# Values and latents paired with gates in two passes of seven half-block products, their weights' sums added up in place by transfers

## The chip, the cores and the metric

The kernel runs on one core of one Trainium2 chip. The metric is the device time of one execution in microseconds (us). Times and profiles come from the chip: the profiler records one execution, and the runs are timed apart from it.

Five engines take part: TensorE (PE, matrix products into PSUM), VectorE (DVE), ScalarE (ACT), GpSimd (POOL) and SyncE (SP). Each runs its own list of instructions in order and stops at the first whose semaphores are not there yet. SP issues nearly all loads; POOL issues the transfers that add to what lies at their target. Sixteen DMA engines move the data.

## The reference: what is computed

One decoder layer on 512 tokens of width 2048, in float32. A normalised input is multiplied by one wide weight, whose columns make all the parts:

```python
h = _rms_norm(x, g_pre)
proj = h @ w_in
(q_lat, kv_lat, k_rope_raw, gate_mla,
 fq, fk, fv, f_logit, gate_fox) = jnp.split(proj, split_points, axis=-1)
o_mla = _mla_branch(q_lat, kv_lat, k_rope_raw, ..., cos, sin) * jax.nn.silu(gate_mla)
o_fox = _fox_branch(fq, fk, fv, f_logit, b_forget) * jax.nn.silu(gate_fox)
o = jnp.concatenate([o_mla, o_fox], axis=-1) @ w_out
return x + _rms_norm(o, g_post)
```

Eight FoX heads (width 128, with forget gates) work on `fq`, `fk`, `fv`, each 1024 wide. Eight MLA heads get their queries, keys and values by a second projection (`w_uq`, `w_ukv`) out of the normalised latents (768 and 512 wide); 64 values of each query and of one shared key are turned by rotary angles, `positions` times a frequency. Both branches are multiplied by SiLU gates of 1024 columns each.

## The kernel before

**Products.** Each float32 number is split into a high part that TensorE takes whole and a low rest, and a product is three matmuls: high by high, high by low, low by high (`mm3`, lines 149 to 152). `h` (`hh`, `hl`) stays in SBUF. Weights come in chunks of 512 KB (128 partitions by 1024 columns, two 128-row blocks of 512 columns or four of 256). `chunk` keeps loads some chunks ahead (`load`, L259 for plain ones, L242 for summed ones); `divide` makes the high part on ACT (`whi`, L279) and the rest on DVE (`wlo`, L282). All chunks of a stage share three places of raw weights in the pool `wp`, with some more in other pools.

**Seven products for eight.** For several groups of columns the product of 2 by 2 half-blocks is done by seven products of sums (names `p1`, `p2`, `p4`, `q6`, `g7`, `g5`, `g3`) in place of eight; `p` ones take blocks of `h`, the others sums of blocks of `h`, which are made once, stored in DRAM (`awaymg`) and fetched again (`bmg`, `bmq`). Before the change these are the FoX values (v), the latents (l), the MLA gates (m), the up-projection (u) and the output (o). The FoX gates are four plain passes, `fg`. The latents are computed turned (weights on the stationary side, so 128 columns by 256 tokens come out and no transposes are wanted later); the MLA gates are not, and are turned afterwards by 32 transposes `gmt`.

**Sums of weights.** A seven-product also wants sums of weight blocks. They are made in DRAM ahead of time: `add_step` copies a block to DRAM with SP (`t7v`, `t6v`, ...) and adds a second one with an accumulating transfer of POOL (L320), paced by `set_pace`. Others are joined on DVE: the second block is loaded beside the first (`second`) and added (`raw<-raw,second`, L269).

**Order.** The start is written out by hand: `proj_first` turns the tokens of `x` (`xt`, by TensorE), makes `h` out of them (ACT the high part, DVE the low part, L145) and uses each of the 16 rows k of `h` at once in the product `in` (L614). `x` and the first weights come in by SP in the order in which they are used. After that a planner orders each engine's instructions by its own estimate of when operands are there, save where `in_order` pins them; smaller work is handed out between the steps of products from a list, `todo`. The rotary tables are such a list: about 25 DVE operations of 128x512, the first of them pinned (L838), in the passes of FoX gates and values.

Of the kernel before, what the change touches and what calls it, by code (L numbers as in the profile page):

```python
# [12 lines left out]
F32 = mybir.dt.float32  # L13
# [6 lines left out]
P = 128  # L20
# [27 lines left out]
DEEP, EXTRA = 6, 3  # L48
# [18 lines left out]
def tile_hybrid_layer(  # L67
# [69 lines left out]
    def split_into(hi, lo, src, scale=None, pin=False):  # L137
        if scale is None:
            a = act.copy(hi, src)
            b = dve.tensor_tensor(out=lo, in0=src, in1=hi.bitcast(F32), op=ALU.subtract)  # L140
            if pin:
                in_order(a, b)
        else:
            act.mul(hi, src, scale)
            dve.scalar_tensor_tensor(  # L145
                out=lo, in0=src, scalar=scale, in1=hi.bitcast(F32), op0=ALU.mult, op1=ALU.subtract
            )

# [70 lines left out]
    raws, ready, up_chunks, early = {}, {}, set(), set()  # L219

    more, deep, seconds = [], [], [vr, 2]
    needs = {}

    def raw_tile(i):
        if deep and deep[1] <= i < deep[2] and (i - deep[1]) % (DEEP + 3) < DEEP:
            return deep[0].tile([P, 1024], F32, tag="raw", name=f"raw{i}", bufs=DEEP)
        if i in up_chunks:
            return slot(f"raw{i}", shape=(P, 1024))
        if i <= prods["g7", "v"][-1] and i % 5 < 2:
            return vr.tile([P, 1024], F32, tag="raw", name=f"raw{i}", bufs=2)  # L230
        pool = more[0] if more and (i - more[1]) % 6 < 3 else wp
        return pool.tile([P, 1024], F32, tag="raw", name=f"raw{i}", bufs=3)

    def load(i, small=None):

        w, cols, k, n, width = chunks[i]
        assert state["step"] >= needs.get(i, -3) + 2
        if cols is None:
# [5 lines left out]
            if k is not None:  # L244
                if seconds and i not in early:
                    pool, bufs = seconds
                    second = pool.tile([P, 2, 512], F32, tag="second", name=f"second{i}", bufs=bufs)
                else:
                    second = slot(f"second{i}")
# [22 lines left out]
    def divide(i):  # L272
# [6 lines left out]
        cast = act.copy(hi[:, :m], raw[:, :m])  # L279
        if deep:  # L280
            tc.keep_in_program_order(cast)
        dve.tensor_tensor(out=lo[:, :m], in0=raw[:, :m], in1=hi[:, :m].bitcast(F32), op=ALU.subtract)  # L282
        ready[i] = [t[:, :m].rearrange("p (k c) -> p k c", k=n) for t in (hi, lo)]

# [7 lines left out]
    def chunk(i, ahead_load=4, ahead=2):  # L292
        upto = i + ahead_load
        if deep:
            upto = max(upto, min(i + DEEP + 2, deep[2] - 1, state["loaded"] + i % 2))
# [4 lines left out]
        for k in range(i + ahead + 1, min(state["loaded"], i + ahead + (3 if deep else 2))):  # L300
            join(k)
# [63 lines left out]
    AT = {"v": O_FV, "l": 0, "m": O_GM}  # L365
# [5 lines left out]

    for g in "vlm":
        sum_blocks(g, lambda j, h, c, g=g: in_block(g, j, h, c), ("t4", "t5"))
# [16 lines left out]
    for n in ("g0", "p1", "g1", "p2", "g2", "s5", "q0", "s3", "k0", "s6", "p4", "s7",  # L390
              "q1", "k1", "q2", "k2", "q3", "k3", "g3"):
        name = {"p1": "p1", "p2": "p2", "p4": "p4", "s5": "g5", "s3": "g3", "s6": "q6", "s7": "g7"}.get(n)
        if name:
            add_products([(name, "v")], plain_in)
            if n == "s5":
                early.update(prods["g5", "v"][2:])
        else:
            at = {"q": O_FQ, "k": O_FK, "g": O_GF}[n[0]] + 256 * (3 - int(n[1]))
            fox[int(n[1])][n[0]] = add_chunks(w_in, [(0, at, 256)], NK, 4, 256)
    add_products(  # L400
        [
            ("p1", "l"), ("p1", "m"), ("p2", "l"), ("p4", "l"), ("p2", "m"), ("p4", "m"),
            ("q6", "l"), ("g5", "m"), ("g7", "l"), ("g5", "l"), ("g3", "l"),
            ("q6", "m"), ("g7", "m"), ("g3", "m"),
        ],
        plain_in,
    )
    mla = [{} for _ in range(4)]
    for n in ("q0", "p1", "k0", "q6", "p2", "p4", "g7", "q1", "g5", "k1", "g3", "q2", "k2", "q3", "k3"):
# [6 lines left out]
        if n[0] == "q":  # L416
            mla[p]["q"] = add_chunks(
                w_uq,
                [
                    (0, 2 * QK * p, NOPE),  # L420
# [1458 lines left out]
```

## Time and profile before

Three runs gave 893.46, 893.65 and 896.54 us; the median is 893.65 us. The profiled execution has a span of 892.3 us.

| what | before |
|---|---|
| span of the profiled execution | 892.3 us |
| median of the runs | 893.65 us |
| TensorE busy | 880.3 us (99%), 4486 matmuls and transposes |
| DVE busy | 660.2 us (74%) |
| ACT busy | 462.1 us (52%) |
| POOL busy | 72.8 us (8%) |
| moved by DMA | 225.07 MB |

Busy time is the share of the span in which an engine had an instruction running; matmuls overlap, so the mean duration of one (some 0.39 us for 128x512) is longer than the distance from one start to the next. That distance is what a matmul costs here, and it is read from the timeline. "PEclk" is the clock granted to TensorE. A window's DMA share is the mean busy share of 16 engines.

### The profile page before, as it was taken

How to read it: one execution, taken by the hardware profiler on the slowest of the kernel's cores; microseconds unless marked ns; L12 is line 12 of the kernel's file. 1: busy time of each engine (PE TensorE's matmuls, PEld its weight loads, DVE VectorE, ACT ScalarE, POOL GpSimd, SP SyncE). 2: the span in 40 equal slices, each digit the busy share in tenths (PEclk: the TensorE clock that was granted, in tenths of full speed). 3: DMA queues.
4: the chain of work that ended last, by engine and by line, in shares of the span. 5: the costliest groups of instructions: out<-in, count | busy, mean ns of one | idle time of the engine just before them, and what ended most of it. 6: DMA issues, size and time to landing. Idle time of an engine off the chain costs nothing.

```text
span 892.3 us, 12700 instructions
## 1 busy us (share of the span) xinstructions
PE 880.3 (99%) x4486; PEld 748.2 (84%) x4486; DVE 660.2 (74%) x1106; ACT 462.1 (52%) x841; POOL 72.8 (8%) x92
## 2 busy tenths in 40 slices
PE   9999999999999999999999999999999999999996
PEld 9988887888888888888998999788888888888885
DVE  4579995648665546477678999979787895988786
ACT  6944434334343433335455565657465776646383
POOL 0110110011110211010000000000000000000021
PEclk9999999999999999999999999999999999999999
DMA  9998798889999999997799885697988637799878
GB/s 319 277 265 241 212 341 279 250 214 315 261 282 275 238 230 225 247 231 186 243 412 410 329 303 178 167 275 166 221 182 215 153 111 233 228 323 322 264 214 254
DMA packets 139235, 225.07 MB, mean 252 GB/s; under 512 B 16898, under 2 KB 68892, under 8 KB 138148
## 3 DMA queue, kind: packets, MB, share of 16 engines
q1 hardware_dynamic: 124660, 184.19, 63.5%
q0 software_dynamic: 13776, 39.85, 22.2%
q8 instruction: 35, 0.57, 0.2%
q10 hardware_dynamic: 736, 0.22, 0.1%
q14 instruction: 28, 0.23, 0.1%
HBM read 209.53 MB, written 69.22 MB: 312 GB/s over the span
## 4 chain that ended last, share of the span: by engine, by line
PE 91%; DVE 4%; DMA 2%; ACT 2%; issue 1%; DVEq 0%; ACTq 0%; SPq 0%
PE fq L150 3%; PE fk L150 3%; PE fk L152 3%; PE fk L151 3%; PE fq L152 3%; PE fq L151 3%; PE fg L150 3%; PE in L614 3%; PE fg L151 3%; PE fg L152 3%; PE sm L657 3%; PE mq L152 2%; PE mq L150 2%; PE mq L151 2%; PE oa L150 2%; PE oa L152 2%
## 5 line engine op out<-in xcount | busy, mean ns | idle before, releaser
L282 DVE TENSOR_TENSOR wlo<-raw,whi 128x1024 fp32r<-128x1024 f32 (+3 forms) x220 | 261.0, 1189 | 134.0 <-ACT whi L279 125.8
L279 ACT CAST whi<-raw 128x1024 fp32r<-128x1024 f32 (+3 forms) x220 | 224.3, 1023 | 233.5 <-PE fk L151 31.8
L150 PE MATMUL fk<-h,whi 128*128 128x512 f32 x128 | 52.6, 411 | 0.0
L150 PE MATMUL fq<-h,whi 128*128 128x512 f32 x128 | 50.9, 397 | 0.0
L150 PE MATMUL fg<-h,whi 128*128 128x512 f32 x128 | 50.3, 393 | 0.0
L152 PE MATMUL fk<-h,wlo 128*128 128x512 f32 x128 | 50.2, 392 | 0.0
L151 PE MATMUL fk<-h,whi 128*128 128x512 f32 x128 | 50.2, 392 | 0.0
L152 PE MATMUL fq<-h,wlo 128*128 128x512 f32 x128 | 50.0, 391 | 0.0
L151 PE MATMUL fq<-h,whi 128*128 128x512 f32 x128 | 49.9, 390 | 0.0
L152 PE MATMUL fg<-h,wlo 128*128 128x512 f32 x128 | 49.9, 390 | 0.0
L151 PE MATMUL fg<-h,whi 128*128 128x512 f32 x128 | 49.9, 390 | 0.0
L675 ACT ACTIVATE pf<-pf,stf 128x128 f32<-128x128 f32 (+3 forms) x32 | 18.0, 562 | 61.4 <-DVE stf L666 61.4
L269 DVE TENSOR_TENSOR raw<-raw,second 128x1024 f32<-128x1024 f32 x32 | 39.0, 1219 | 0.5 <-DMA second<-in_w_out_dram 0.5
L614 PE MATMUL in<-whi,h 128*128 128x328 f32 x128 | 30.0, 321 | 0.0
L150 PE MATMUL mq<-ln,whi 128*128 128x512 f32 x72 | 29.2, 406 | 0.0
L152 PEld LDWEIGHTS fk<-h,wlo 128*128 128x128 f32 x128 | 24.1, 188 | 5.5
L152 PEld LDWEIGHTS fq<-h,wlo 128*128 128x128 f32 x128 | 24.0, 188 | 5.3
L152 PEld LDWEIGHTS fg<-h,wlo 128*128 128x128 f32 x128 | 24.0, 188 | 5.2
L151 PE MATMUL mq<-ln,whi 128*128 128x512 f32 x72 | 28.3, 393 | 0.0
L152 PE MATMUL mq<-ln,wlo 128*128 128x512 f32 x72 | 28.2, 392 | 0.0
L151 PEld LDWEIGHTS fg<-h,whi 128*128 128x128 f32 x128 | 24.1, 188 | 4.7
L150 PEld LDWEIGHTS fg<-h,whi 128*128 128x128 f32 x128 | 24.1, 188 | 4.7
(610 smaller groups left out, 2417.5 us busy)
## 6 DMA issues: line engine op xcount, KB each, us to landing
raw<-in_w_in_dram SPq DMA_DIRECT2D x96, 512.0 KB
raw<-in_w_out_dram SPq DMA_DIRECT2D x32, 512.0 KB
second<-in_w_in_dram SPq DMA_DIRECT2D x24, 512.0 KB
bmg<-awaymg SPq DMA_DIRECT2D x20, 256.0 KB
awaymg<-rmg POOLq DMA_DIRECT2D x8, 512.0 KB, 6.8
raw<-t6v SPq DMA_DIRECT2D x8, 512.0 KB
t7o<-in_w_out_dram SPq DMA_DIRECT2D x4, 1024.0 KB
t7o<-in_w_out_dram POOLq DMA_DIRECT2D x4, 1024.0 KB, 10.6
```

What stands on the lines that cost most here:

```text
L150: pe.matmul(o, ah, bh, start=first, stop=False, **kw)
L151: pe.matmul(o, ah, bl, start=False, stop=False, **kw)
L152: pe.matmul(o, al, bh, start=False, stop=last, **kw)
L269: tc.keep_in_program_order(dve.tensor_tensor(out=raw, in0=raw, in1=second, op=ALU.add))
L279: cast = act.copy(hi[:, :m], raw[:, :m])
L282: dve.tensor_tensor(out=lo[:, :m], in0=raw[:, :m], in1=hi[:, :m].bitcast(F32), op=ALU.subtract)
L614: pe.matmul(banks[t][:, :n], a[k][:, tss[t]], b[:, j, :], start=k == 0 and m == 0, stop=k == NK - 1 and m == 2,)
L657: pe.matmul(s[:, :nn], a[:, qs], c[:, :nn], start=(i == 0), stop=(i == len(pairs) - 1))
L675: act.activation(p, p, AF.Exp, bias=st[:, 0:1], scale=unit, accum_out=st[:, 1:2])
```

## The change: what it does

The FoX gates join the seven-products (group g), so that two passes remain that each handle two groups, step by step in turn: "vg" for values and FoX gates, "lm" for latents and MLA gates. The groups g, l and m are computed turned, so the 32 transposes `gmt` go. The SiLU of the gates is computed later, head by head, from `todo`.

The sums of weights of v, g, l and m are no longer made in DRAM or on DVE. A raw place is filled, divided, and then filled again where it stands: `follow` names the chunk that comes after chunk i in the same place, and `divide` issues at its end a plain load by SP, an accumulating transfer by POOL, or both. One place thus goes through B11, +B12, B22 afresh, +B12, +B11, +B21.

The rotary tables are computed on tiles of 128x128: four small transfers bring the positions, DVE takes the same steps on a quarter of the columns, three sines are made on ACT, and the result goes to DRAM (`tables`) and from there to the tables in eight transfers. The pin on the first operation is gone. The FoX queries of the first pair are computed at the place where the first pass of FoX gates was; the probabilities of the attention are normalised on ACT and not on DVE.

```diff
+    def fill(i, raw):
+        raws[i] = raw
+        to = raw.rearrange("p (k c) -> p k c", k=2)
+        first, second = chunks[i][0]
+        if first is not None:
+            nc.sync.dma_start(to, first)
+        if second is not None:
+            pool.dma_start(to, second, accum_op=ALU.add)
...
         dve.tensor_tensor(out=lo[:, :m], in0=raw[:, :m], in1=hi[:, :m].bitcast(F32), op=ALU.subtract)
         ready[i] = [t[:, :m].rearrange("p (k c) -> p k c", k=n) for t in (hi, lo)]
+        if i in follow:
+            fill(follow[i], raw)
...
+    B11, B12, B21, B22 = ((h, c) for h in range(2) for c in range(2))
+    REST = ("g3", B22, None), ("g7", None, B12), ("q6", None, B11), ("p4", None, B21)
...
+    add_fox(0, "q")
+    add_chain("vg", "p1", B11, None)
+    add_plain("vg", "p2", *B21)
+    for g in "vg":
+        up_chunks.update(prods["p2", g])
+    for step in (("g5", None, B12), *REST):
+        add_chain("vg", *step)
...
+    add_plain("lm", "p1", *B11)
+    add_plain("lm", "p2", *B21)
+    for j in range(1, 4):
+        chain["m", j] = prods["p2", "m"][j]
+    for step in (("g5", B11, B12), *REST):
+        add_chain("lm", *step)
...
-            dve.tensor_scalar(out=p, in0=p, scalar1=st[:, 2:3], scalar2=None, op0=ALU.mult)
+            act.mul(p, p, st[:, 2:3])
...
-        pi = vr.tile([P, S], I32, tag="c", name="pos")
-        nc.sync.dma_start(pi, positions.to_broadcast([P, S]))
+        rows = cst.tile([P, 3, P], F32, name="angles")
+        r, n1, n2 = (rows[:, i, :] for i in range(3))
+        for b in range(NT):
+            nc.sync.dma_start(
+                r[32 * b : 32 * (b + 1), :].bitcast(I32),
+                positions[:, b * P : (b + 1) * P].to_broadcast([32, P]),
+            )
...
-            in_order(dve.tensor_copy(n1, pi))
+            dve.tensor_copy(n1, r.bitcast(I32))
             dve.tensor_scalar(out=r, in0=n1, scalar1=ifc[:, 0:1], scalar2=None, op0=ALU.mult)
...
+            act.activation(n2, r, AF.Sin, scale=-1.0)
             dve.scalar_tensor_tensor(out=n1, in0=r, scalar=-1.0, in1=r, op0=ALU.mult, op1=ALU.max)
-            act.activation(cosT, n1, AF.Sin, scale=-1.0, bias=half)
+            act.activation(r, r, AF.Sin)
+            act.activation(n1, n1, AF.Sin, scale=-1.0, bias=half)
+            pool.dma_start(to, rows.rearrange("p n c -> p (n c)"))
...
+    def products(gs, between, out=lambda g, c, half: None):
+        G, C, B = {}, {}, {}
+        for name in ("g5", "g3", "g7", "q6", "p4"):
+            for g in gs:
...
+                one(name, g, bank_of[g], name in ("g5", "g7", "p4"), rate, side)
+                if name == "g5":
+                    place(g, 1, 1)
+                    put(g, 1, 1, G[g], ALU.subtract, P1)
...
+    rot = rotary_tables()
+    todo.append(fs[0])
+    todo.extend([*x_steps(0), *x_steps(1)])
+    places = [(g, j) for g in "vg" for j in range(4)]
+    for g, j in places[:5]:
+        fill(prods["p1", g][j], vr.tile([P, 1024], F32, tag="raw", name=f"raw{g}{j}", bufs=5))
+    q0 = fox_q(0, [att_bank("fq00"), bank("pv", "fq01", 1)], v_block)
...
+    products(
+        "vg",
+        {
+            ("g5", "v"): (1, d3), ("g5", "g"): (1, f7), ("g5", "g", "after"): lambda: todo.extend(rot),
```

The order of the instructions moves more than these lines tell. Two places matter for what follows.

At the start, DVE makes the low parts of `h` (one `h` row for each k, from the turned tokens `xt`) and of the first weights (`wlo`). Before, from its row for k = 2 on:

```order
L145 SCALAR_TENSOR_TENSOR h_284<-xt_279,gcol,h_284 128x512
L282 TENSOR_TENSOR wlo_288<-raw_183,whi_287 128x656
L145 SCALAR_TENSOR_TENSOR h_312<-xt_307,gcol,h_312 128x512
L145 SCALAR_TENSOR_TENSOR h_336<-xt_331,gcol,h_336 128x512
L282 TENSOR_TENSOR wlo_340<-raw_190,whi_339 128x656
```

With the change, the same place on DVE (h_233 is k = 2, h_261 k = 3, h_285 k = 4; `angles` is the tile of positions and angles):

```order
L142 SCALAR_TENSOR_TENSOR h_233<-xt_228,gcol,h_233 128x512
L283 TENSOR_TENSOR wlo_237<-raw_135,whi_236 128x656
L870 CAST angles<-angles 128x128
L871 TENSOR_SCALAR angles<-angles,ifc 128x128
L877 TENSOR_SCALAR angles<-angles 128x128
L878 TENSOR_SCALAR angles<-angles 128x128
L142 SCALAR_TENSOR_TENSOR h_261<-xt_256,gcol,h_261 128x512
L885 SCALAR_TENSOR_TENSOR angles<-angles 128x128 x4
L877 TENSOR_SCALAR angles<-angles 128x128
L878 TENSOR_SCALAR angles<-angles 128x128
L142 SCALAR_TENSOR_TENSOR h_285<-xt_280,gcol,h_285 128x512
L283 TENSOR_TENSOR wlo_289<-raw_142,whi_288 128x656
```

The rotary list that stood behind the third product of the values now stands on DVE in the middle of the first rows of `h`, its first operation ahead of the row for k = 3.

On SP, the transfers that bring the positions stand in this place (xa are the loads of `x`, the last is xa_162; the words in brackets are the semaphores that SP waits for, which are those of the eighth transfer before):

```order
L178 DMA xa_150<-in_x_dram 128x4x256 [waits DMAHW0_49]
L178 DMA xa_155<-in_x_dram 128x4x256 [waits DMAHW1_49]
L178 DMA xa_160<-in_x_dram 128x4x256 [waits DMAHW2_49]
L178 DMA xa_162<-in_x_dram 128x4x256 [waits DMAHW3_49]
L766 DMA bcol<-in_b_forget_dram 8x1 [waits DMAHW4_49,Pool_49]
L859 DMA ifc<-in_inv_freq_dram 128x2 [waits DMAHW5_49]
L863 DMA angles<-in_positions_dram 32x128 [waits DMAHW6_49]
L863 DMA angles<-in_positions_dram 32x128 [waits DMAHW7_49]
L863 DMA angles<-in_positions_dram 32x128 [waits DMAHW0_49]
L863 DMA angles<-in_positions_dram 32x128 [waits DMAHW1_49]
```

The order before had there, with two more weight chunks of the start (raw_200, raw_205) ahead of the last loads of `x`:

```order
L179 DMA xa_208<-in_x_dram 128x4x256 [waits DMAHW6_49]
L179 DMA xa_210<-in_x_dram 128x4x256 [waits DMAHW7_49]
L735 DMA bcol<-in_b_forget_dram 8x1 [waits DMAHW0_49,Pool_49]
L828 DMA ifc<-in_inv_freq_dram 128x2 [waits DMAHW1_49]
L830 DMA pos<-in_positions_dram 128x512 [waits DMAHW2_49]
```

So the positions are asked for behind all of `x` in both kernels; before, the first DVE operation on them stood a long way down the list. Two chunks that were loaded ahead of the last `x` now come behind the positions.

The second place is POOL, at the head of the pass lm (rawl, rawm and raw are places of raw weights of l and m; awayoa and awayog carry the sums for the output product). With the change:

```order
L993 DMA awayoa_4761<-gc_1106 256x1x256
L237 DMA rawl_4335<-in_w_in_dram 128x2x512
L237 DMA rawl_4338<-in_w_in_dram 128x2x512
L237 DMA rawl_4341<-in_w_in_dram 128x2x512
L237 DMA rawl_4344<-in_w_in_dram 128x2x512
L237 DMA raw_4420<-in_w_in_dram 128x2x512
L993 DMA awayoa_4907<-gc_1105 256x1x256
L993 DMA awayog_4832<-rog_4817 128x1024
L993 DMA awayog_4868<-rog_4853 128x1024
L237 DMA rawm_4578<-in_w_in_dram 128x2x512
```

Every L237 row adds 512 KB to a place in SBUF; 64 of them stand on POOL in the whole program (32 for each pass), where before 24 adds of 512 KB went to DRAM for v, l and m.

More of the change, by code (lines that the diff above doesn't have):

```diff
@@ L244, in load @@
             if k is not None:
[L245 to L249, printed above, removed]
+                second = slot(f"second{i}")
                 nc.sync.dma_start(second, k)
```

556 lines of the change are left out of this document (261 added, 295 removed).

## The prediction

> **What bounds the kernel now.** I read the page's busy times first, then its chain of waits.
>
> ```profile
> span 892.3 us, 12700 instructions
> PE 880.3 (99%) x4486; PEld 748.2 (84%) x4486; DVE 660.2 (74%) x1106; ACT 462.1 (52%) x841; POOL 72.8 (8%) x92
> ...
> PE 91%; DVE 4%; DMA 2%; ACT 2%; issue 1%; DVEq 0%; ACTq 0%; SPq 0%
> ```
>
> TensorE bounds it: 99% of the span, 91% of the chain. So an edit is worth what it adds to or takes from TensorE's own work and TensorE's waits. Neither saved DVE time nor saved bytes count by themselves. A wait of TensorE early on is never made up, since no later stretch has slack for it.
>
> **Term 1, TensorE's work.** The price of a matmul is the distance between starts, which the timeline of TensorE shows.
>
> ```profile
> 51.42 0.39 PE L152 MATMUL fg<-h,wlo 128*128 128x512 f32 x1
> ...
> 54.14 0.39 PE L152 MATMUL fg<-h,wlo 128*128 128x512 f32 x1
> ...
> 499.80 0.28 PE L150 MATMUL gcl<-bmq,whi 128*128 128x256 f32 x1
> ...
> 502.92 0.28 PE L152 MATMUL gcl<-bmq,wlo 128*128 128x256 f32 x1
> ...
> 589.27 0.87 PE gmt L1441 x8
> ```
>
> From 51.42 to 54.14 stand 12 starts: 0.227 us for 128x512. From 499.80 to 502.92 stand 26: 0.120 us for 128x256. A gate transpose is 0.87/8 = 0.109. Removed: four passes `fg` of 96 wide matmuls (384), the 336 wide ones of the MLA gates, and 32 transposes: 720 x 0.227 + 32 x 0.109 = 163.2 + 3.5 = 166.7 us. Added: seven products of 96 narrow ones each for g and for m, 1344 x 0.120 = 161.3 us. The term is **-5.4 us**. Both pitches are steady over long rows, so I give it only 1 us either way.
>
> **Term 2, the start.** DVE now has the first rotary operation ahead of its low part of `h` for k = 3, in an engine that takes its instructions in order. What is queued behind it is that row, then the row and the weights' rest for k = 4, and TensorE's `in` products want them all. So the question is when the positions land. These are the rows of DVE, TensorE and SP before:
>
> ```profile
> 12.28 0.75 DVE L145 SCALAR_TENSOR_TENSOR h<-xt,gcol,h 128x512 fp32r<-128x512 f32 x1 [0.74 <-ACT h L144]
> 14.52 0.75 DVE L145 SCALAR_TENSOR_TENSOR h<-xt,gcol,h 128x512 fp32r<-128x512 f32 x1 [1.48 <-ACT h L144]
> 15.18 0.83 DVE L282 TENSOR_TENSOR wlo<-raw,whi 128x656 fp32r<-128x656 f32 x1
> ...
> 13.16 0.60 PE L499 MATMUL xt<-ident,xa 128*128 128x128 f32 x4
> 13.51 1.43 PE L614 MATMUL in<-whi,h 128*128 128x328 f32 x8
> ...
> 16.39 0.31 PE L614 MATMUL in<-wlo,h 128*128 128x328 f32 x1
> ...
> 13.89 1.92 SPq L179 DMA_DIRECT2D xa<-in_x_dram  x2
> 15.92 0.38 SPq L735 DMA_DIRECT2D bcol<-in_b_forget_dram  x1
> 16.35 0.37 SPq L828 DMA_DIRECT2D ifc<-in_inv_freq_dram  x1
> 16.76 0.42 SPq L830 DMA_DIRECT2D pos<-in_positions_dram  x1
> ...
> 21.88 0.88 SPq L259 DMA_DIRECT2D raw<-in_w_in_dram  x2
> ...
> 15.00:20.00 5.00, 5.00 (x39) 4.98 (x38) 3.30 (x6) 4.91 (x18) 0.00 (x0) 1.00 1.10 374
> ```
>
> Before, the low part for k = 3 is done at 12.28 + 0.75 = 13.0. TensorE starts k = 3 at 13.51, and its fifth matmul is the first to want that part, at about 13.51 + 4 x 0.15 = 14.1.
>
> The positions stand behind all of `x`. SP's row at 21.88 waits in its order for the last load of `x`, so that landed at about 21.8. Positions issued at 16.76 lie behind it on the same 16 engines, full in this window (share 1.10, 374 GB/s); the transfer that waits for them in SP's order starts at about 23.2, so they landed between 21.9 and 23.2, some 0.7 us after `x`. The changed order puts two chunks of 328 KB behind, not ahead: 0.67 MB at 374 GB/s, 1.8 us earlier. So the angles land at 21.9 + 0.7 - 1.8, about 20.5 (20.1 to 21.4).
>
> DVE then does four operations of 128x128 before the row for k = 3.
>
> ```profile
> 560.85 0.87 DVE L531 TENSOR_SCALAR lrkdl<-ident,lrkl 128x128 fp32r<-128x128 f32 x4
> L819 DVE TENSOR_TENSOR nk<-nk,mask 128x128 f32<-128x128 f32 x24 | 5.5, 284 | 0.0
> ```
>
> At 0.22 to 0.28 each that is 1.0 us, and 0.75 for the row: done at 22.2, against the 14.1 at which TensorE wants it. That is 8.1 us of TensorE doing nothing. Then six more operations (1.5 us), the row for k = 4 (0.7) and `wlo` (0.8): 25.2, where TensorE used that `wlo` at 16.39 before. The delay is **8.8 us**. From k = 5 the rest of the rotary work, 15 more small operations, fits beside TensorE: a k takes it 2.2 us, and DVE has 3.30 busy of 5.00. ACT, which gets three sines in the same stretch, is at 4.91 of 5.00; they may cost up to 1 us more. I take **+9.0**. From below, if the positions overtook the queued loads and landed 2 us after their issue, near 18.5, it would be 6.5; if they did not hold DVE at all, 0. From above it is 10.5.
>
> One more thing hangs on a stall of that length. At the end of the program, where TensorE has run dry, the clock falls:
>
> ```profile
> 885.00:889.00 4.00, 0.91 (x2) 0.30 (x2) 3.17 (x9) 0.88 (x2) 0.24 (x1) 1.00 0.89 309
> 889.00:892.30 3.30, 0.00 (x0) 0.00 (x0) 0.00 (x0) 0.00 (x0) 0.00 (x0) 0.57 0.48 171
> ```
>
> Granted is 1.00 and then 0.57. The Trainium skill, "TensorE: Matmul & The Clock Gate", section "Part 1: The HAM clock gate", says that about 3.4 us without work halve the clock, and that as much sustained work brings it back; the end of the trace agrees in that the clock falls only after some time of idling. By it the start would lose up to 1.7 us more, part of it inside TensorE's second wait; by the row of the steady start, nothing. An estimate by that page is +1 us.
>
> **Term 3, stalls that go.** The old sums cost DVE a join, and twice TensorE waited for a divide that stood behind other DVE work.
>
> ```profile
> 136.83 1.22 DVE L269 TENSOR_TENSOR raw<-raw,second 128x1024 f32<-128x1024 f32 x1
> 139.29 3.50 DVE L282 TENSOR_TENSOR wlo<-raw,whi 128x1024 fp32r<-128x1024 f32 x3 [1.24 <-ACT whi L279]
> 139.31 0.50 PE L150 MATMUL vg<-whi,smg 128*128 128x512 f32 x1 [0.89 <-ACT whi L279]
> 140.57 0.50 PE L151 MATMUL vg<-wlo,smg 128*128 128x512 f32 x1 [0.76 <-DVE wlo L282]
> ...
> 557.00:577.00 20.00, 19.10 (x88) 15.19 (x87) 18.24 (x41) 11.54 (x18) 0.88 (x1) 1.00 0.68 155
> ```
>
> 0.89 + 0.76 = 1.65 in the pass of values, and 0.90 of the 20 us of latents and gates. With 24 of the 32 joins gone and the MLA gates' evacuation moved, both should go: **-2.6 us** (0 if they move only).
>
> **Term 4, the adds in place.** 64 adds of 512 KB go to SBUF, 32 in each pass, where 24 went to DRAM. A place cannot be filled before it is divided, and the next product wants it: a late add is now a wait of TensorE, while sums in DRAM were made hundreds of microseconds ahead.
>
> ```profile
> q1 hardware_dynamic: 124660, 184.19, 63.5%
> q0 software_dynamic: 13776, 39.85, 22.2%
> ...
> t7v<-in_w_in_dram POOLq DMA_DIRECT2D x4, 512.0 KB, 8.3
> ...
> 866.00:870.00 4.00, 4.00 (x19) 3.34 (x18) 1.97 (x2) 3.85 (x6) 2.70 (x4) 1.00 1.01 170
> 475.00:485.00 10.00, 10.00 (x46) 8.29 (x45) 9.02 (x11) 6.51 (x8) 0.00 (x0) 1.00 1.03 410
> ```
>
> POOL's queue q0 took 22.2% of 892.3 = 198 us of all engines for 39.85 MB, 2.6 us for 0.524 MB. Where adds alone fill the engines (866 to 870) they move 170 GB/s, 3.1 us each; plain loads (475 to 485) 410 GB/s, 1.3 us. I take 2.8. A step of a pass is one product for both groups: for vg 48 x 0.227 + 96 x 0.120 = 22.4 us of TensorE, with eight adds, 8 x 2.8 = 22.4. The three steps with adds one after the other (`g7`, `q6`, `p4`) follow the step of `g3`, whose refills are plain loads of 8 x 1.3 = 10.4; that leaves 12 us of lead, from which go the fetches of `sums`. It just fits in vg. At the head of lm it doesn't: POOL's adds for `g5` compete with the plain loads of `p2`, whose three places are refilled only as they come free, at 11.5/4 = 2.9 us a chunk against a landing of 8 us and more; and the first add for the gates stands behind another add and three transfers of heads. Bounds: 0, if the lead suffices; above, one landing of 8.3 late in either pass, with another 10% of six steps of adds (6 x 22.4 x 0.1), about 15 in all (the fetches squeezed in). Nearest is the lead that just fits: a few waits of 1 to 2 us, **+4**.
>
> The Trainium skill, "DMA: Bandwidth & Descriptors", section "Anatomy of one DMA", fits a POOL transfer by 2.0 us and its bytes over 436 GB/s: 3.2 us for 512 KB, of which 1.2 would be engine time. The landing of 8.3 us and the 170 GB/s disagree; the fit was not made for adding transfers. By it this term would be 0 and the sum 4 us less.
>
> **What costs nothing.** The normalisation of probabilities moves from DVE (about 64 operations) to ACT, which is half idle (52%). If ACT were not idle there, a score block's chain would grow by about 0.5 us; heads lie behind products with 4 us steps. The turned groups save bytes and joins that TensorE did not wait for.
>
> **Sum.** The profiled execution has 892.3 of span, and the median of the runs is 1.35 above it. 892.3 + 1.35 - 5.4 + 9.0 - 2.6 + 4 = 898.7; I say **899**.
>
> **Rivals.** (a) *The start does not stall.* For it: the positions are only 64 KB, and small packets may pass between large ones. Against: SP's row at 21.88 and the engines at share 1.10. Then 893.65 - 5.4 - 2.6 + 0 to 4 = 886 to 890: faster. (b) *The start stalls and the adds fit.* For it: the lead of 12 us in each pass, and DVE freed of joins. Against: the head of lm. 893.65 - 5.4 + 9.0 - 2.6 = 894.6 (893 to 896): no change, the gain being eaten by the wait. (c) *The adds become the bound.* Place: q0 in the last three steps of each pass; it decides from the point where an add takes more than 22.4/8 = 2.8 us with the fetches between. At the 3.1 us of the window, 24 adds lose 24 x 0.3 = 7 us, and 12 to 15 in two passes: 907 to 910, clearly slower. For it: the window 866 to 870. Against: the average of q0, 2.6.
>
> **How the numbers follow.** A measurement of this kernel can tell 0.5% (4.5 us) from no change: faster is below 889.2, slower above 898.1. My forecast (start stalls, adds cost 2 to 8: 896 to 903) 0.46; (a) 0.17, (b) 0.20, (c) 0.17. Faster: nearly all of (a) and little else, 0.16. No change: (b), a third of the forecast's chance below 898.1, 0.34. Slower 0.50. The range reaches from (a) at its best, 886, to (c), 909; the forecast's own is 895 to 903.
>
> **What would show it.** After, DVE's cast on the angles should wait for a DMA from about 12 to 20.5 us, and TensorE should have a hole of 8 us before its first `in` product of k = 3 with low parts, and another of about 1 us at k = 4; with no hole there, term 2 is wrong and (a) holds. The granted clock behind the hole shows whether the gate fell. TensorE's busy time summed over pitches should be 5 us less. In vg and lm, waits of TensorE for `whi` or `wlo` whose own releaser is a DMA show term 4; POOL's adds should land 8 us and more after issue, and their DMA share should be near 1. Waits for ACT in the attention would show that the moved normalisation is not free.

## The result, and the profile after

The changed kernel takes 919.58 us in the median of four runs (915.59 to 922.15), the kernel before 893.56 (893.41 to 896.54): a ratio of 1.028, with a 95% interval of 1.024 to 1.032. The forecast was 899, slower by 0.6%, with a range up to 909; it was slower by 2.8%. The profiled execution has a span of 920.4 us, 28.1 more than before; its run, 922.15 us, is the longest of the four, so the holes read from it are in sum up to 6.6 us larger than in the shortest.

The page of the changed kernel: busy times, TensorE's clock by slices, the chain of waits, and the two big DMA queues.

```profile
span 920.4 us, 13773 instructions
PE 885.9 (96%) x5078; PEld 779.2 (85%) x5078; DVE 634.6 (69%) x1056; ACT 499.4 (54%) x914; POOL 125.4 (14%) x133
...
PEclk8899989999999999899999999999999999999998
...
q1 hardware_dynamic: 101300, 136.28, 46.7%
q0 software_dynamic: 26256, 61.02, 33.5%
...
PE 79%; DMA 10%; DVE 4%; issue 3%; ACT 2%; POOL 1%; SPq 1%; DVEq 0%; ACTq 0%; POOLq 0%
```

Three things are to be seen. TensorE still sets the end, but its share of the chain fell from 91% to 79%, and DMA's rose from 2% to 10%: the waits are for transfers now. POOL's queue took 33.5% of 920.4 = 308 us of all engines in place of 198. And the clock, which the page of before shows at 9 tenths or more in every slice, has slices at 8 at the start and in the middle.

To see where the 28 us are, I took from the traces the distance from each matmul's start to the next, less the usual (median) distance of its shape, and summed it by stage. I call this TensorE's lost time; it holds waits and also matmuls at a slower clock. What is left of the span is TensorE's work: 892.3 - 18.2 = 874.1 before, 920.4 - 51.7 = 868.7 after.

| TensorE's lost time, us | start, to the first `va` | values (and gates) | FoX heads | latents and gates | MLA heads, output, end | sum |
|---|---|---|---|---|---|---|
| before | 2.9 | 2.7 | 2.4 | 2.4 | 7.8 | 18.2 |
| after | 15.7 | 6.6 | 8.7 | 8.9 | 11.8 | 51.7 |
| difference | +12.8 | +3.9 | +6.3 | +6.5 | +4.0 | +33.5 |

So the work became 5.4 us less, and lost time 33.5 us more. Five places hold most of that.

**The start.** Windows of the changed kernel (stretch and length in us; busy time and number of instructions of PE, PEld, DVE, ACT and POOL; clock; DMA share; GB/s):

```profile
14.00:18.00 4.00, 1.32 (x10) 1.04 (x9) 0.00 (x0) 2.12 (x6) 0.00 (x0) 0.98 1.10 347
18.00:22.00 4.00, 0.00 (x0) 0.00 (x0) 0.00 (x0) 0.00 (x0) 0.00 (x0) 0.50 0.65 169
22.00:26.00 4.00, 1.94 (x7) 1.94 (x8) 3.45 (x12) 0.00 (x0) 0.00 (x0) 0.50 0.98 314
26.00:30.00 4.00, 4.00 (x24) 3.94 (x23) 3.60 (x8) 2.38 (x7) 0.00 (x0) 0.74 0.95 338
```

Its timeline there, rows of SP's queue, DVE and TensorE (start, length, instruction, and the idle time ahead with what ended it):

```profile
15.56 3.27 SPq L863 DMA_DIRECT2D angles<-in_positions_dram  x4
...
22.27 0.23 DVE L870 CAST angles<-angles 128x128 f32<-128x128 int32 x1 [9.80 <-DMA angles<-in_positions_dram]
...
24.06 1.46 PE L645 MATMUL in<-whi,h 128*128 128x328 f32 x4 [8.74 <-DVE h L142]
```

The positions were asked for between 15.56 and 18.83 us. The cast on them held DVE for 9.80 us, until 22.27, and TensorE stood for 8.74 us. The clock fell to 0.50 in that time, and came back between 26 and 30 us.

**The FoX heads, at 370 us.** The changed kernel's timeline, rows of SP's queue, ACT and TensorE:

```profile
345.44 4.80 SPq L262 DMA_DIRECT2D raw<-in_w_in_dram  x1
353.69 0.24 SPq L327 DMA_DIRECT2D t4o<-whi  x1
357.78 0.38 SPq L262 DMA_DIRECT2D raw<-in_w_in_dram  x1
...
370.38 1.04 ACT L282 CAST whi<-raw 128x1024 fp32r<-128x1024 f32 x1 [4.70 <-DMA raw<-in_w_in_dram]
...
371.75 1.06 ACT L282 CAST whi<-raw 128x1024 fp32r<-128x1024 f32 x1
371.75 0.38 PE L149 MATMUL pvf<-phf,fv2h 128*128 128x256 f32 x1 [2.30 <-ACT phf L138]
...
375.46 0.63 PE L151 MATMUL fq<-h,wlo 128*128 128x512 f32 x1
375.88 0.63 PE L149 MATMUL fq<-h,whi 128*128 128x512 f32 x1
```

And its windows:

```profile
370.00:375.00 5.00, 2.31 (x7) 1.79 (x8) 3.42 (x6) 3.78 (x8) 0.00 (x0) 0.78 0.99 281
372.90:379.60 6.70, 6.53 (x18) 5.30 (x19) 6.24 (x18) 1.84 (x5) 1.57 (x2) 0.50 0.97 269
```

The weight chunk of SP's row at 345.44, asked for by 350.24, was there for ACT only at 370.38, 20 us later, and the next one, asked for at 357.78, at 371.75, 14 us later. The cast of `phf` for an older head stood behind the first of these casts on ACT. After a wait of 2.30 us and one of 0.94 TensorE ran at half speed for nearly 7 us (0.42 us from start to start in place of 0.227).

**The head of lm, at 504 us.** Of the changed kernel's timeline, rows of POOL and ACT:

```profile
488.03 1.23 POOL L237 DMA_DIRECT2D rawm<-in_w_in_dram  x1 [0.91 <-DMA rawm<-in_w_in_dram]
...
503.07 1.04 ACT L282 CAST whi<-rawm 128x1024 fp32r<-128x1024 f32 x1 [11.85 <-DMA rawm<-in_w_in_dram]
```

Of its waits (who waits for whom: sum in us, number, longest), and then of its windows:

```profile
PE mg L149 <- ACT whi L282: 5.3, 1, 5.3
```

```profile
440.00:450.00 10.00, 10.00 (x83) 9.87 (x82) 6.95 (x17) 8.09 (x17) 0.00 (x0) 1.00 0.46 128
490.00:495.00 5.00, 5.00 (x44) 5.00 (x43) 2.22 (x2) 1.13 (x2) 1.78 (x2) 1.00 1.07 337
500.00:505.00 5.00, 0.80 (x2) 0.50 (x2) 0.85 (x1) 1.93 (x2) 0.00 (x0) 0.75 1.10 260
```

The first add for the gates was issued at 488.03 and its chunk was there at 503.07: 15 us. TensorE waited 5.3 us. The engines were full in the windows from 490 us on; from 440 to 450 they had been half idle.

**The other two** are the second product of vg (105 to 125 us), where TensorE waited 2.4 us for one `wlo` and less for others, at half speed for nearly 7 us after, and the first MLA heads (625 to 645 us), where it lost 3.5 us, 2.0 of them in short waits.

### The profile page after: what moved, and what is told of

The parts are those of the page before. It is cut to its first block, busy times and chain, and to the rows that moved or that the text cites. A ratio compares the mean times of both kernels' runs of the same rounds, so it can differ in the third digit from the quotient of the medians.

```text
span 920.4 us, 13773 instructions
## 1 busy us (share of the span) xinstructions
PE 885.9 (96%) x5078; PEld 779.2 (85%) x5078; DVE 634.6 (69%) x1056; ACT 499.4 (54%) x914; POOL 125.4 (14%) x133
## 3 DMA queue, kind: packets, MB, share of 16 engines
q0 software_dynamic: 26256, 61.02, 33.5%
## 4 chain that ended last, share of the span: by engine, by line
PE 79%; DMA 10%; DVE 4%; issue 3%; ACT 2%; POOL 1%; SPq 1%; DVEq 0%; ACTq 0%; POOLq 0%
DMA raw<-in_w_in_dram 4%; DMA rawm<-in_w_in_dram 3%; PE sm L688 3%; PE fq L149 3%; PE in L645 3%; PE fq L150 3%; PE fq L151 3%; PE fk L151 2%; PE fk L149 2%; PE fk L150 2%; PE mq L149 2%; PE mq L150 2%; PE mq L151 2%; PE sf L688 2%; PE oa L151 2%
## 5 line engine op out<-in xcount | busy, mean ns | idle before, releaser
L283 DVE TENSOR_TENSOR wlo<-raw,whi 128x1024 fp32r<-128x1024 f32 (+3 forms) x159 | 186.8, 1177 | 116.7 <-ACT whi L282 116.0
L282 ACT CAST whi<-raw 128x1024 fp32r<-128x1024 f32 (+3 forms) x159 | 160.6, 1012 | 153.7 <-PE fk L150 33.7
L282 ACT CAST whi<-rawv 128x1024 fp32r<-128x1024 f32 x24 | 25.1, 1050 | 41.5 <-PE gc L150 9.8
L282 ACT CAST whi<-rawg 128x1024 fp32r<-128x1024 f32 x24 | 25.2, 1051 | 29.7 <-PE vc L151 8.9
L283 DVE TENSOR_TENSOR wlo<-rawv,whi 128x1024 fp32r<-128x1024 f32 x24 | 29.3, 1224 | 17.1 <-ACT whi L282 17.0
L283 DVE TENSOR_TENSOR wlo<-rawg,whi 128x1024 fp32r<-128x1024 f32 x24 | 29.3, 1223 | 14.2 <-ACT whi L282 14.2
L282 ACT CAST whi<-rawl 128x1024 fp32r<-128x1024 f32 x20 | 21.0, 1049 | 22.2 <-PE mc L150 7.5
L283 DVE TENSOR_TENSOR wlo<-rawl,whi 128x1024 fp32r<-128x1024 f32 x20 | 24.4, 1223 | 10.2 <-ACT whi L282 10.2
L645 PEld LDWEIGHTS in<-whi,h 128*128 128x128 f32 x128 | 22.0, 193 | 9.4 <-DVE h L142 9.0
L149 PE MATMUL mq<-ln,whi 128*128 128x512 f32 x72 | 29.0, 403 | 0.0
L150 PEld LDWEIGHTS fq<-h,whi 128*128 128x128 f32 x128 | 24.7, 193 | 4.5
```

Source lines behind the costliest of these rows:

```text
L149: pe.matmul(o, ah, bh, start=first, stop=False, **kw)
L150: pe.matmul(o, ah, bl, start=False, stop=False, **kw)
L645: pe.matmul(banks[t][:, :n], a[k][:, tss[t]], b[:, j, :], start=k == 0 and m == 0, stop=k == NK - 1 and m == 2,)
```

## The experiments

In all of them the kernel before was run on the same chip beside them. All ratios below are to it.

### One cause taken away at a time

**e1: the angles later.** One line puts the pin back.

```diff
-            dve.tensor_copy(n1, r.bitcast(I32))
+            in_order(dve.tensor_copy(n1, r.bitcast(I32)))
```

> The changed kernel with the first rotary operation pinned in program order again, so that the whole list of angles stands on DVE behind the sixth product of the pass vg and no longer among the first rows of h; nothing else is edited. Theory H (the hole at the start is made by DVE standing in front of the positions, and nothing later gives it back): TensorE's lost time in the first 50 us falls from 14.5 us to the 3 us of before, and the span from 920.4 to about 909, the other holes staying where they are. Rival: the start is late anyway or the later stretches (loads, adds) are late by what is won, so that less than 6 us remain: 914 or more.

Measured: 910.06 us, a ratio of 1.016 (1.013 to 1.019), a span of 908.9. The span is the one expected of theory H, but by luck: the start lost 7.4 us, not 3, and some 4 us of the gain stand in later stages that the theory did not count (values and gates 6.6 to 5.1, FoX heads 8.7 to 6.5; the table is below). At the start a second wait, which the first had covered, came out. ACT of this kernel:

```profile
27.19 0.74 ACT L282 CAST whi<-raw 128x656 fp32r<-128x656 f32 x1 [4.00 <-DMA raw<-in_w_in_dram]
```

The sixth weight chunk of the start was late. It is one of the two that I had counted as moved behind the positions, to their gain; that they would be late themselves I had not followed, since with the first hole they are not.

**e2: the sums in DRAM slower.** `set_pace(3.7)` becomes `set_pace(6)` ahead of the FoX heads (before the change 4.9 stood there).

> The changed kernel with the pace of the sums in DRAM (u and output) set to 6 steps in place of 3.7 in the FoX stage. Theory D (the hole of 6.9 us at 370 us is a weight chunk that lands 14 us after its issue because 1 MB adds and copies fill the DMA engines and SP's eight outstanding transfers): the hole goes, the span falls by about 7 to 913.5. Rival: the chunk's own place comes free too late: the hole stays at 5 to 7 us with the span at 920.

Measured: 912.84 us, 1.019 (1.016 to 1.022), span 911.6. The FoX heads lost 2.0 us, against 8.7 in the changed kernel and 2.4 before the change; the other 2.1 us of the gain stand in stages that the edit does not touch. Windows of this kernel:

```profile
360.00:370.00 10.00, 10.00 (x50) 8.24 (x50) 5.00 (x8) 4.18 (x8) 0.67 (x2) 1.00 0.74 160
370.00:380.00 10.00, 10.00 (x48) 8.35 (x47) 8.02 (x25) 5.18 (x12) 2.01 (x3) 1.00 0.93 275
```

TensorE is busy all through, and the DMA share is 0.74 where it was full. The hole at 370 us was made by the pace of copies and adds of 1 MB, a number that the change had altered and that no term of the prediction speaks of.

**e3: no adds in place.**

```diff
-        if second is not None:
-            pool.dma_start(to, second, accum_op=ALU.add)
```

> The changed kernel without the 64 adding transfers of POOL into raw places (this part of the computation is left out, the weights' sums are then wrong); loads, divides and products are all there. Theory E (the adds fill the DMA engines and POOL's queue, and chunks and stores behind them come late): the hole at 504 us (8.3) goes, that at 105 to 125 us falls from 6.6 to the 2.5 of DVE's long reciprocal; the holes at the start (11.5 over before) and at 370 us (6.9) stay. Span about 908. Rival: the two holes are made by the order on DVE, ACT and SP, and the adds are hidden: 918 or more.

Measured: 904.64 us, 1.010 (1.007 to 1.013), span 902.6, 18 us under the changed kernel. Latents and gates lost 0.3 us in place of 8.9, values and gates 0.7 in place of 6.6, and the FoX heads 5.4 in place of 8.7 (why these lost less is open). Of this kernel's waits, the one in the second product of vg, and POOL's queue on its page:

```profile
PE ga L151 <- DVE wlo L281: 0.4, 1, 0.4
q0 software_dynamic: 8848, 27.46, 13.5%
```

POOL's queue took 13.5% of 902.6 = 122 us of all engines, against 308 with the 64 adds: 2.9 us for each.

DVE's long reciprocal, to which I had put 2.5 us, costs next to nothing once the chunks are there in time. Theory E holds, with more on it than expected: the adds, or what queues behind them, make the loss in both passes.

**e4: e1 and e2 together.**

> Both edits at once, the angles later and the slower pace of the sums in DRAM. If holes of TensorE simply add up, since it has no slack anywhere: 920.4 - 11.5 - 6.9, a span of about 902. Rival: winning time early makes the transfers of the later stages late, and the second edit gives less than half of its 7 us: 906 or more.

Measured: 905.81 us, 1.012 (1.010 to 1.014), span 903.6. The two edits gave 11.5 and 8.8 us alone and 16.8 together. Most adds up. Of the 3.5 us that are missing, the start lost 1.4 more than in e1 (the late chunk, now uncovered, cost 6.1 us between 25 and 50 us here, 4.4 in e1), and the 2.2 us that e1 had gained in the FoX heads could not be gained a second time.

### Step by step towards a kernel without the holes

Each of these is the one before it with one more edit.

**e5: places for two chunks of the start.** `up_chunks` begins as `{5, 6}`, so the sixth and seventh chunk take places that are free at once.

> The kernel of e4 with places of their own for the sixth and seventh weight chunk of the start, so that SP asks for them ahead of the last loads of x as before the change. Theory S (behind the hole of the positions a second one was hidden: these chunks are loaded behind positions and 1 MB of weights for a later product, and TensorE waits for them at 28 us): the 6 us lost between 25 and 50 us go to under 1, span from 903.6 to about 898.5. Rival: the chunks are then on time but the raw weights behind them are late, and a hole of the same size opens before 100 us: 902 or more.

Measured: 903.26 us, 1.009 (1.005 to 1.012), span 902.4. The wait for the chunk at 28 us is gone, and a third one stands in its place. A row of this kernel's waits:

```profile
PE rrow L570 <- issue: 2.8, 1, 2.8
```

The row of norms (`rrow`) comes late, at 49 us. The gain was 1.2 us of span (2.5 between the medians) where I expected 5: the rival was nearer. Three waits stood behind one another here.

**e6: the stores of sums of `h` ahead of the first adds.** A list `held` keeps the fills of the first product's places, and two are issued, in program order, at each divide of the second product. The edit's core, without the lines that set `hold` and pin the order:

```diff
         if i in follow:
-            fill(follow[i], raw)
+            held.append((follow[i], raw))
+        for _ in range(0 if state["hold"] else min(2, len(held))):
+            fill(*held.pop(0), pin=i in prods["p2", "v"] or i in prods["p2", "g"])
```

> The kernel of e5, with the first eight adds of the pass vg issued later, in the course of the second product, so that the stores of the sums of h stand ahead of them on POOL. Theory P (chunks of the second product wait for places that the stores leave, and the stores wait behind the adds): the 5 us lost between 100 and 125 us fall to 2.5 (DVE's long reciprocal stays), span about 896. Rival: the adds are then late themselves for the third product: the loss moves to 125 to 160 us and the span stays at 898 or more.

Measured: 904.04 us, 1.010 (1.007 to 1.013): no gain. Theory P falls in this form. POOL's and ACT's rows of this kernel's timeline, and then two of its windows, tell why:

```profile
90.34 2.52 POOL L238 DMA_DIRECT2D rawv<-in_w_in_dram  x2
91.81 5.92 POOL L238 DMA_DIRECT2D rawg<-in_w_in_dram  x4
...
104.98 1.05 ACT L285 CAST whi<-raw 128x1024 fp32r<-128x1024 f32 x1 [4.50 <-DMA raw<-in_w_in_dram]
109.42 1.05 ACT L285 CAST whi<-raw 128x1024 fp32r<-128x1024 f32 x1 [2.42 <-DMA raw<-in_w_in_dram]
113.41 1.05 ACT L285 CAST whi<-raw 128x1024 fp32r<-128x1024 f32 x1 [2.94 <-DMA raw<-in_w_in_dram]
```

```profile
85.00:90.00 5.00, 5.00 (x44) 5.00 (x43) 3.41 (x5) 2.09 (x2) 0.57 (x2) 1.00 0.30 113
110.00:115.00 5.00, 3.97 (x29) 3.33 (x27) 2.42 (x3) 2.06 (x3) 0.00 (x0) 1.00 1.11 261
```

The held adds went out together, six in 4 us after a stretch at a share of 0.30, and then the plain chunks came 4.4 and 4.0 us apart, at 261 GB/s. That is 1.05 MB in 4.0 us, one add and one plain load: at 1.3 us for the load, as the prediction had it, 2.7 are left for the add. TensorE uses a chunk every 2.9 us. So, by this estimate, a burst of adds delays each load that comes after it by about a microsecond more.

**e7: the latents' loads half a product earlier.** The four fills of the latents' third product move from behind the first products of both groups to between them.

> The kernel of e6, with the loads of the four raw places of the latents' third product issued half a product earlier, between the first product of l and that of m. Theory L (at the head of lm 50 us of full DMA engines follow 20 us of engines half idle; the last add, for the first chunk of the gates, lands 15 us after its issue): the 7.8 us lost near 488 us fall to 3 or less, span about 891. Rival: that add is late by its own queue (an add and three stores ahead of it on POOL, its place late): the loss stays above 6, span 895 or more.

Measured: 899.12 us, 1.005 (1.004 to 1.007), span 897.1. The loss in this stage fell from 8.9 to 4.8 us (to 6.8 in e8, which has the same instructions there), and it moved: the wait at 488 us is gone, and one for ACT's `phf` stands at 445 us, behind a cast that waits for a plain chunk among the four adds. That fits the same burst in another place; e9 tests it.

**e8: the first gates behind the scores.**

> The kernel of e7, with the gates of the first two MLA heads computed behind these heads' scores and not ahead of their keys. Theory G (the 3 us lost near 620 us come from the gates' DVE and ACT work, about 5 us with a table load, that now stands among the work that the first scores wait for): loss below 1.5, span 2 us less than e7. Rival: the first scores wait for the rotation of the queries, whatever the gates do: same as e7 within 0.7 us.

Measured: 898.90 us, 1.005 (1.003 to 1.007): the same as e7. The loss of the last stages fell from 11.3 to 10.3 us, and the first scores still wait for the queries' rotation (`rq`, 1.3 us). The rival is right but for 1 us; most of that loss is left open. The loss in the latents and gates, 2.0 us higher than in e7, hides the gain in the span.

**e9: the adds spread in time.** `divide` issues one held fill each time from the middle of the first products on; the latents' four fills are issued by `side` steps, one by one over three products.

```diff
+    def early(j):
+        return lambda: fill(prods["g5", "l"][j], slot(f"rawl{j}", shape=(P, 1024)), True)
...
+        one("p1", g, A[g], side=[none, none, early(0), none] if g == "l" else [early(1), none, early(2), none])
```

> The kernel of e8, but the adds are spread in time: in vg one add for each divide from the middle of the first pair of products on, in lm the four loads and adds of the latents' third product one by one over three products. Theory B (it is the burst that hurts: an add and a plain load of 512 KB together take the engines 2.8 + 1.3 = 4.1 us, and chunks are used every 2.9 us, so in a burst each plain load is late by about a microsecond more): the 5.3 us lost between 100 and 125 us fall to about 2, the 6.7 lost near 446 us to about 2, span about 889, level with or just under the kernel before. Rival: the sum of transfers in these stretches is too much whatever the order: the losses move but keep their size, span 895 or more.

Measured: 895.12 us, 1.0013 (0.9998 to 1.0028), span 894.6. Latents and gates lost 1.7 us (0.7 and 1.6 in e10 and e11, with the same instructions there): there theory B holds. Values and gates lost 6.2, no less: two of the stores stood among the adds on POOL again, and a chunk waits for a place that such a store leaves.

**e10: the adds of vg behind all stores, one for each divide.**

> The kernel of e9, with the adds of vg behind all eight stores of the sums of h, one for each divide of the second pair of products, two of them only in the third. Theory Q (in e9 the loss at 106 us is a chunk whose place came free when a store landed 10 us after its issue, behind three adds): the 6.2 us lost between 100 and 125 us fall below 3, span about 891. Rival: 16 plain loads and eight adds in these 45 us leave no room, the loss stays at 5 us or moves to the third product: span 894 or more.

Measured: 894.44 us, 1.000 (0.998 to 1.002), span 892.0. Values and gates lost 3.2 us (3.3 in e11). The stores first did not do it with six adds in a row behind them (e6, 5.2 us), nor the adds spread with stores among them (e9, 6.2 us). Here the adds were not spread as the edit meant: four left POOL within 2.2 us behind the last store, at 89.82 to 92.00 us, and two at 108.36 and 109.11. What took effect is then a shorter burst behind the stores; which of its parts matters more was not tested.

**e11: the first fills tied to DVE's work.** Five loads of 512 KB that SP had put ahead of the chunks of the start follow small writes that DVE makes during the first FoX queries.

```diff
+    def first_fill(g, j):
+        raw = vr.tile([P, 1024], F32, tag="raw", name=f"raw{g}{j}", bufs=5)
+        in_order(dve.memset(raw[:, 0:1], 0.0))
+        fill(prods["p1", g][j], raw)
```

> The kernel of e10, with the loads of the first five raw places of vg tied to small writes that DVE makes in the course of the first FoX queries, so that these 2.6 MB no longer stand ahead of the chunks of the start and of these queries. Theory R (the 3.6 us lost between 25 and 75 us are a chunk that lands late because of these loads, in front of the work that the row of norms waits for): the loss falls below 1.5, span about 889.5, the time some 0.3 to 0.5% under the kernel before. Rival: the fills are then late for the first product of the values, a hole of 2 us or more opens near 62 us, span 891 to 894.

Measured: 891.25 us in the median of 12 runs (889.50 to 891.84) beside 894.03 for the kernel before: 0.9953 (0.9937 to 0.9970), a little faster than both. Two lines of its page, and two of its windows:

```profile
span 889.8 us, 13786 instructions
PE 875.5 (98%) x5078; PEld 771.9 (87%) x5078; DVE 633.0 (71%) x1061; ACT 500.4 (56%) x914; POOL 125.5 (14%) x133
```

```profile
125.00:425.00 300.00, 300.00 (x1670) 261.25 (x1669) 180.89 (x336) 143.07 (x252) 49.67 (x48) 1.00 0.87 208
425.00:500.00 75.00, 74.22 (x605) 73.03 (x604) 48.43 (x66) 40.18 (x60) 17.45 (x17) 1.00 1.04 303
```

From 125 to 425 us TensorE is never idle, and from 425 to 500 for 0.8 us. Between 25 and 75 us it lost 0.1 us, where the kernels from e5 to e10 lost 1.7 to 3.7: theory R holds in its numbers. The table of lost time over the steps:

| us lost | start | values, gates | FoX heads | latents, gates | rest | sum | span |
|---|---|---|---|---|---|---|---|
| after | 15.7 | 6.6 | 8.7 | 8.9 | 11.8 | 51.7 | 920.4 |
| e1 angles later | 7.4 | 5.1 | 6.5 | 9.6 | 11.2 | 39.8 | 908.9 |
| e2 slower sums | 14.9 | 5.2 | 2.0 | 9.4 | 11.3 | 42.9 | 911.6 |
| e3 no adds | 15.9 | 0.7 | 5.4 | 0.3 | 11.3 | 33.5 | 902.6 |
| e4 e1 and e2 | 8.8 | 4.9 | 2.0 | 8.1 | 11.3 | 35.2 | 903.6 |
| e5 start chunks | 6.2 | 5.4 | 2.1 | 8.7 | 11.4 | 33.7 | 902.4 |
| e6 stores first | 6.8 | 5.2 | 2.0 | 8.9 | 11.3 | 34.2 | 903.3 |
| e7 latents early | 4.8 | 5.6 | 2.1 | 4.8 | 11.3 | 28.5 | 897.1 |
| e8 gates behind | 4.3 | 5.2 | 2.0 | 6.8 | 10.3 | 28.6 | 897.3 |
| e9 adds spread | 5.7 | 6.2 | 2.0 | 1.7 | 10.4 | 26.1 | 894.6 |
| e10 adds between | 6.2 | 3.2 | 2.0 | 0.7 | 10.5 | 22.6 | 892.0 |
| e11 first fills later | 3.7 | 3.3 | 2.0 | 1.6 | 10.6 | 21.2 | 889.8 |

In every row the span less the sum lies between 868.4 and 869.4: TensorE's work is the same in all, and all that the edits moved is lost time. Between kernels that have the same instructions in a stage, its lost time differs by up to 2.5 us in the start (4.3 to 6.8 from e5 to e10) and up to 2.0 in the latents and gates (e7 and e8), and by some tenths in the FoX heads with the slower pace. Single profiles go no finer than that; the steps on which the account rests, in the start from 15.7 to 7.4, in the FoX heads from 8.7 to 2.0 and in the two passes from 15.5 to 1.0 without the adds, are well above it.

## Why the prediction was wrong, by its own steps

**The bound** was right. TensorE had no slack, and a wait was not made up: e1, e2 and e3 gave 11.5, 8.8 and 17.8 us of span for 11.9, 8.8 and 18.2 us of lost time, and no stage after the one that was mended lost the gain again.

**Term 1, -5.4 us of work,** was right to the tenth: 874.1 to 868.7.

**Term 2, +9.0 us at the start,** named the right instruction, place and cause, and was too small: the start lost 12.8 us more. Its sum for the landing, 21.9 + 0.7 - 1.8, is 20.8 and not 20.5, and the positions were used at 22.27. The load that SP issued at 21.41 waits in its order for the last of `x`; so `x` landed 0.4 us earlier than before, where I had put 1.8, and the third and fourth transfer of the positions waited on SP for earlier loads of `x` (1.5 us). The low part for k = 3 was done at 24.0, not 22.2; but TensorE too came to its wait later than put, at 15.3 and not at 14.1 (24.06 less 8.74). So the stall was 8.74 for 8.1: two errors that nearly cancel. The wait at k = 4, 0.7 us of the term, did not come. What the term left out are about 2.2 us of matmuls at half clock behind the stall, a wait of 1.1 us for `x` at 8.5 us, and one of 0.9 us for `rrow` at 58 us.

The Trainium skill, "TensorE: Matmul & The Clock Gate", section "Part 1: The HAM clock gate", gives about 3.4 us without work and as much sustained work to get back. The trace agrees in part: TensorE stood from 15.3 us, the clock shows 0.98 in the window up to 18 us and 0.50 from 18 on, so it fell after some 2.6 us; work began at 24.06, and the clock shows 0.74 from 26 to 30 and 1.00 after. But shorter waits made the clock fall too (the last section), so 3.4 us are not needed here. I had it as an extra of 1 us, kept out of the sum.

**Term 3, -2.6 us,** did not come: the two old stalls went, and the adds made larger ones in their stages. In e3, without the adds, the two passes lost 1.0 us where 5.1 stood before.

**Term 4, +4 us, is the step that failed.** Values and gates together with latents and gates lost 15.5 us where 5.1 stood before: 10.4 more, or 13.0 if the term 3 gain is counted as given back; about 5.2 of the 10.4 are matmuls at half clock behind the two waits. The price of an add was right: e3 gives 2.9 us, e6's spacing 2.7, POOL's queue with 110 us more for 21.2 MB more 2.7, for the 2.8 that I took. What was wrong is where I priced it. I worked out the load of the steps with nothing but adds, late in a pass, called it a fit, and there TensorE waits for nothing: the changed kernel's window

```profile
160.00:180.00 20.00, 20.00 (x135) 18.51 (x134) 12.60 (x14) 9.12 (x11) 8.34 (x8) 1.00 1.10 222
```

has full engines and 20.00 of 20 us of TensorE. The loss is at the head of each pass, where the first adds meet plain loads for the second product, with three places and no lead, and stores whose places those loads want. For lm I named this place and the very add (the first one for the gates, behind another add and three stores), and then put "a few waits of 1 to 2 us" on it, with one late landing of 8.3 us in the upper bound. It landed after 15 us. A landing read from a stretch with few adds is not the landing in a queue of them: by these prices, as an estimate, each add in front adds its 2.8 us and each load its 1.3. The upper bound was summed wrong besides: 8.3 + 13.4 is 21.7, not 15. The loss lies within either; the step that failed is the choice of +4 between the bounds, by a fit that was worked out for the wrong stretch.

The Trainium skill, "DMA: Bandwidth & Descriptors", section "Anatomy of one DMA", fits a POOL transfer of 512 KB with 3.2 us, of which, as an estimate, 1.2 are for its bytes. By that there would have been no loss; for adding transfers the runs contradict it, with 2.9 us of all engines for each add and with 17.8 us of span between e3 and the changed kernel.

**No term** spoke of the pace of the sums in DRAM: 3.7 for 4.9 stands in the diff, and I read it as part of the new order. That stage lost 6.3 us more (e2: 8.7 to 2.0). None spoke of the gates' move into the MLA heads either. From the MLA heads on the program lost 4.0 us more; e8 brings back 1.0, and what makes up the other 3 stays open. The measured 919.58 less these 10.3 would be 909.3, at the upper end of the range.

**What I left out in all of them** is the clock behind a wait. The waits at 118 and 371 us, 2.8 and 3.2 us long, lost 5.8 and 6.9 us. Behind the four large holes the clock stood at 0.50, and the matmuls in these stretches lost about 2.2 (start), 2.7 (118 us), 3.5 (371 us) and 2.5 us (504 us), together 11 of the 33.5. In the changed kernel 90 matmuls (of 128x256 and wider) stand at 1.6 to 2.05 times their usual distance, for 9.9 us in sum; before, 21 for 2.2.

**The rivals.** (a), no stall at the start, is refuted by the cast's 9.80 us. (b), stall and fitting adds, by e3. (c), the adds as the bound, had the right cause and the wrong place (the last three steps) and stopped at 910. The sum with what was measured: 892.3 - 5.4 + 12.8 (start) + 3.9 + 6.3 + 6.5 + 4.0 = 920.4. Of the 23.1 us by which this is above the forecast's own sum of spans (897.3), term 4 is short by 6.4, the pace by 6.3, the rest by 4.0, the start by 3.8 and term 3 by 2.6.

## What to carry to other kernels

Where one engine has no slack, price a transfer by the stretch in which it runs and not by its stage's mean: list what else the queues carry there, how many places its readers have, and what stands ahead of it in the same queue. Count with a wait the slow clock behind it, here 2 to 3.5 us for each large one. Behind one wait look for the next: here three stood behind one another at the start, and taking away the first gave 7 of 12 us. When a pin on an order is taken off, read the new order at the places where an engine now stands in front of a late transfer, and read a changed pace as a change.

## What the runs showed of the hardware that I had not expected

Short waits already cost the clock. Two windows of the changed kernel, and one of the kernel before:

```profile
115.00:116.80 1.80, 0.50 (x2) 0.30 (x2) 1.77 (x2) 1.80 (x4) 0.52 (x1) 1.00 0.41 150
116.90:123.60 6.70, 5.61 (x26) 5.61 (x27) 5.78 (x7) 1.80 (x3) 0.82 (x2) 0.50 0.62 197
```

```profile
138.00:142.00 4.00, 2.35 (x9) 1.40 (x8) 2.76 (x4) 2.94 (x3) 0.00 (x0) 1.00 0.66 200
```

After a wait of 0.40 us, and 1.3 us into one of 2.4 us, the clock fell to 0.50 and stood there to 123.6 us, though TensorE was working again from 118 us on. After waits of 2.30 and 0.94 us within 4 us it was 0.50 from 372.9 to 379.6; TensorE was then working nearly all the time, 0.42 us a matmul in place of 0.227. In the kernel before, two waits of 0.89 and 0.76 us within 2 us at 139 us left it at 1.00. What between these waits is enough for a fall, no run here shows.

An add holds the engines about twice as long as a plain load of the same size: 2.9 us (e3) against 1.3. With a queue of adds outstanding, one add and one load of 512 KB went through every 4.0 to 4.4 us (261 GB/s at a share of 1.11), where plain loads alone had run at 410 GB/s. And small transfers wait with the large ones: the four of the positions, 16 KB each, were asked for between 15.56 and 18.83 us, behind `x`, whose last load landed at about 21.4; DVE had them at 22.27.
